# Hybrid encoder trunk, layer 0: where modulation steps and the key's products stand, and how many units of w_out stay plain

## The chip, the cores and the metric

The kernel runs on one core of a Trainium2 chip. The metric is the device time of one execution in microseconds (us). Below, TensorE is the matmul engine (PE, with PEld for its weight loads), VectorE is DVE, ScalarE is ACT, GpSimd is POOL, and SP issues the DMAs. SBUF is the memory on the chip in which all operands lie, PSUM the one that matmuls write.

## The reference

Two layers work on 256 positions of 2048 features. Each layer has this form:

```
mod = silu(c) @ w_mod[l] + b_mod[l]          # six rows of 2048: shift, scale, gate, twice
h = layer_norm(x) * (1 + scale_m) + shift_m
proj = h @ w_in[l]                           # 4288 columns, parts of four mixers
y = concat(y_a, y_b, y_c, y_d)               # gMLP, latent attention, short conv, long conv
x = layer_norm(ALPHA * x + (1 + gate_m) * (y @ w_out[l])) * g + b
h = layer_norm(x) * (1 + scale_f) + shift_f
x = layer_norm(ALPHA * x + (1 + gate_f) * conv_ffn(h)) * g + b
```

In the attention mixer (y_b), a part of `proj` is a latent for the queries, one for keys and values, and 64 columns for the key's rotary part. The latents are normalised and multiplied by a gain; the key part is turned by cosines and sines: `k_rope = k_r * cos + rotated(k_r) * sin`.

## The kernel before

All matrices are float32. A **plain** (in the code: exact) product multiplies float32 operands as they are; its weights are loaded straight into tiles `wexact` of 512 KB. A **split** product cuts each operand into a high half (a cast to float32r by ScalarE, `whi`, line 390) and a low half (what is left, by VectorE, `wlo`, line 391) and makes three products of them (hi by hi, hi by lo, lo by hi). Its weights first land in a tile `wraw` of 1 MB. The tiles `wexact` of most groups live in the same eight buffers as `whi` and `wlo` (four each, line 93). The tiles `wraw`, the weights of the modulation (`wmod`), the rows of gains and biases (`gb`) and the gMLP's parameters share four buffers of 1 MB (`rawp`, line 92).

In **layer 0** the projection is plain. Its last two groups are B (latents, lines 488 to 519) and C (short conv, lines 412 to 461), each of eight units of two k-tiles; C may load two units ahead. The out stage (`out_proj`, line 607) then multiplies the concatenated mixers by w_out in three column chunks: 1024 columns in eight units of two k-tiles (chunk 0), then 512 and 512 columns in four units of four k-tiles each (chunks 1024 and 1536, by their first column). In layer 0 the chunks 1024 and 1536 are plain, and of chunk 0 the first `PLAIN_UNITS` units (line 736). In the last chunk all products of the first 128 positions come ahead of those of the other 128, so that the first tile's norm (line 665) runs beside the second tile's products. That norm needs two rows `gb`, loaded with the last unit's weights (`gains`, line 643), and sums of one of them, made by ScalarE.

**The modulation** is made by VectorE, beside everything else. Each step loads 1 MB of w_mod and takes one instruction over 128x2048 (line 194 for shifts and scales, line 205 for gates). The steps stand in one stream (`mods`, line 305) in a fixed order. A pace sets how many come at a time: each unit adds the rate of its phase (`RATES`, line 35) to a credit, and takes as many steps as the credit has whole parts (`pump`, line 314). The steps of layer 0's feed-forward shift and scale are the last that the out stage's end needs.

**The order.** SP issues all DMAs in one order; an engine runs its instructions in one order; both orders are fixed when the program is built, by a scheduler that takes the instructions in the order of the code as far as their inputs and buffers are ready in its own estimate of the time. `add_manual_dep` adds a fixed order between two instructions. In `run` (line 547) a unit's load is issued before the products of the unit before it, then come the products, the pump and some background pieces (`bg`). The end of group B (`mix_b`, line 1009) squares and copies the latents, and takes `MODS_AHEAD` steps at once (line 1025). The attention (`attend`, line 1062) begins one unit later: it turns the latents on TensorE (`ps_q`, `ps_kv`), makes the key's two products with cosines and sines on VectorE (`kc`, lines 1085 and 1086) and the scaled latents (`kvr`, line 1090). The first of the two kc, and both kvr, are ordered behind the last of the `MODS_AHEAD` steps (`behind`, line 1066). TensorE then adds the key's two products (`ps_kr`) and makes the queries (`ps_qn`). Two PSUM buffers are shared by all these small products (`msp`, line 99), so ps_qn takes over the buffer that the two kvr have read. Beside this the long convolution of mixer D runs: ScalarE scales (line 876), VectorE adds (`convD`, line 879).

Of the kernel before, what the change touches and what calls it, by code (L numbers as in the profile page):

```python
# [9 lines left out]
AF = mybir.ActivationFunctionType  # L10
ALU = mybir.AluOpType
# [4 lines left out]
S = 256  # L16
# [9 lines left out]
C_UV, C_Q, C_SB, C_SC, C_AG = 0, 1024, 1728, 2240, 3264  # L26
# [6 lines left out]


RATES = [
    dict(B=1.3, attend=1.3, C=1.9, out=1.0, out_next=1.55, out_last=0.0, up=0.7, down=0.7, down_next=0.7, down_last=0.0),
    dict(D=1.0, U=0.0, V=0.0, B=0.0, C=0.0, E=0.9, attend=0.0, out=0.6, out_next=0.6, out_last=0.0, up=0.3, down=0.7, down_next=0.7, down_last=0.0),
]

STEPS = [  # L40
    dict(B=1, C=6, out=2, up=2),
    dict(U=7, B=4, C=4, E=8, out=0, up=2),
]

PLAIN_UNITS = 2

MODS_AHEAD = 3

BATCHES = ((0, 4), (4, 4), (8, 4), (12, 4))

# [36 lines left out]
def encoder_kernel(ctx: ExitStack, tc: tile.TileContext, A: dict, consts: bass.AP, out: bass.AP):  # L87
    nc = tc.nc
    pe, act, dve, pool = nc.tensor, nc.scalar, nc.vector, nc.gpsimd
# [41 lines left out]
    sinT = cst[:, 768:1024]  # L131
# [50 lines left out]


    MOD = {}
    last_step = [None]
    data_dep = mybir.DependencyInfo(mybir.DependencyClass.Sync, mybir.DependencyReason.DATA)
    order_dep = mybir.DependencyInfo(mybir.DependencyClass.NoSync, mybir.DependencyReason.DATA)

# [11 lines left out]
    def mod_step(acc, w, kt, first):  # L200
        col = cact[:, kt : kt + 1]
        if first:
            i = dve.tensor_scalar(out=acc, in0=w, scalar1=col, scalar2=None, op0=ALU.mult)
        else:
            i = dve.scalar_tensor_tensor(out=acc, in0=w, scalar=col, in1=acc, op0=ALU.mult, op1=ALU.add)  # L205
        held(i, "mod")
        last_step[0] = i.ins.name

    def gate_rows(l, m, acc):

# [115 lines left out]


    pending = []
    postponed = []
    background = []  # L330

# [189 lines left out]
    hN, first = [], []  # L521
# [22 lines left out]
        for u in range(KT // 4):  # L544
            pump()

    def run(g, ahead=0):
        units, load, products, end, bg = g
        loaded = []

        def get(u):
            while len(loaded) < min(u + 1 + (ahead if u > 0 else 0), units):
                loaded.append(load(len(loaded)))
            return loaded[u]

# [51 lines left out]
    def out_proj(l, stage, w, src, order, gate_of, name, post_g, post_b, before, then, plain=(), bg=0):  # L607
# [112 lines left out]
        for c0, width in CHUNKS:  # L720
            last = c0 + width == D
            nk = 2048 // width
            units = nkt // nk
# [8 lines left out]
            def load_unit(u, c0, width, nk, units, last):  # L732
                kt = order[nk * u]
                assert order[nk * u : nk * u + nk] == list(range(kt, kt + nk))
                spare = nk if last and units - 4 <= u < units - 2 else 0
                exact = c0 in plain or (bool(plain) and u < PLAIN_UNITS)
                parts = weights(w, kt, nk, c0, width, exact, spare)
                s4 = src(kt // 4)
                if exact:
                    return parts, [(s4[:, kt % 4 + k, :], None) for k in range(nk)]  # L740
# [55 lines left out]
    def mixers(l, w_in, Y, hF=None, first_mod=None, quarter=None):  # L796
# [265 lines left out]
        def attend(WQ, WKV, lat, q01, rr):  # L1062
# [20 lines left out]
            by = turn(ps, S, [lat[t][:, 256:320] for t in range(2)])  # L1083
            kc = tmp_tile("kc")
            behind(dve.tensor_tensor(out=kc[0:64, 0:S], in0=by[0:64, :], in1=cosT[0:64, :], op=ALU.mult))
            dve.tensor_tensor(out=kc[0:64, S : 2 * S], in0=by[0:64, :], in1=sinT[0:64, :], op=ALU.mult)
            ps = ms_tile("ps_kv")
            for j in range(2):
                by = turn(ps, j * S, [lat[t][:, j * P : (j + 1) * P] for t in range(2)])
                behind(dve.tensor_scalar(out=kvr[:, j, :], in0=by, scalar1=KVG(j), scalar2=None, op0=ALU.mult))  # L1090

            rope = slot("rope").rearrange("p (j s) -> p j s", j=4)
            ps = ms_tile("ps_kr")
# [211 lines left out]
    def by_blocks(l, w_in, hF, first_mod, quarter, mix_d, mix_u, gelu_v, mix_v, mix_b, mix_c, mix_e):  # L1305
# [94 lines left out]
            mix_c(cps, tps)  # L1400
            mix_e(sumE, None)

        run(group(w_in, C_SC, 1024, f"C{l}", mix_ce, hF=hf, bg=STEPS[l]["C"]), 2)


    def ffn_up(l, G):
# [280 lines left out]
```

## Time and profile before

| | |
|---|---|
| three runs | 2218.09, 2219.70, 2219.76 us; median 2219.7 |
| the profiled execution | 2218.06 us, its span 2216.3 us |
| mean granted clock of TensorE | 0.998 |
| busy: TensorE, VectorE, ScalarE | 2192.1, 1716.9, 1092.7 us |
| moved by the DMA engines | 603.96 MB, mean 273 GB/s |

The span is the time from the first to the last instruction that the profiler saw. A row of a timeline gives the start, the duration of the group, engine, line, operation, output and inputs with their shapes, and how often (x); in brackets stand the idle time of the engine before it and what ended it. A row of stretches gives, for a window of time, its length and the busy time of PE, PEld, DVE, ACT and POOL, each with a count of instructions, then the granted clock, the share of the DMA engines and their GB/s. A row of DMA landings gives the count, the KB of each and the us from issue to landing.

### The profile page before, as it was taken

What the parts mean: (1) busy time and instruction counts of PE and PEld (TensorE: products, weight loads), DVE (VectorE), ACT (ScalarE), POOL (GpSimd) and SP (SyncE); (2) the same over time, 40 slices, a digit from 0 to 9 for tenths busy, and PEclk for the clock granted to TensorE, in tenths of its full rate; (3) what the DMA queues carried; (4) which work ended last, traced back from release to release, by engine and by line L of the source; (5) the groups of instructions that cost most, each with busy time, mean ns of one, the idle gap of its engine ahead of it and who ended that gap; (6) DMA issues with size and microseconds to landing.
All of it is one profiled execution on the core that took longest, in us unless ns stands there. A gap on an engine that the chain in (4) does not pass through costs nothing. (4 is left out here: it accounts for less than half of the span.)

```text
span 2216.3 us, 28397 instructions
## 1 busy us (share of the span) xinstructions
PE 2192.1 (99%) x10880; PEld 1801.1 (81%) x10880; DVE 1716.9 (77%) x2209; ACT 1092.7 (49%) x1677; POOL 21.9 (1%) x38
## 2 busy tenths in 40 slices
PE   9999999999999999999999999999999999999997
PEld 6776875588888888888867988868888888888886
DVE  5658996799888888989968988877766656565776
ACT  3132740655555545545665555465455545454453
POOL 0000000000000000000000000000000000000000
PEclk9999999999999999999999999999999999999999
DMA  9999889588888888888758547856755555555553
GB/s 393 417 374 390 338 330 391 224 331 316 327 315 322 325 328 316 319 329 323 282 208 297 186 156 263 320 197 247 265 210 188 182 198 190 190 190 190 192 192 148
DMA packets 94034, 603.96 MB, mean 273 GB/s; under 512 B 10565, under 2 KB 10693, under 8 KB 29125
## 3 DMA queue, kind: packets, MB, share of 16 engines
q1 hardware_dynamic: 93898, 602.15, 74.0%
q8 instruction: 85, 1.39, 0.2%
q14 instruction: 51, 0.42, 0.1%
HBM read 600.01 MB, written 2.10 MB: 272 GB/s over the span
## 5 line engine op out<-in xcount | busy, mean ns | idle before, releaser
L390 ACT CAST whi<-wraw 128x1024 fp32r<-128x1024 f32 (+1 forms) x608 | 634.5, 1047 | 677.0 <-PE g_c L115 207.8
L391 DVE TENSOR_TENSOR wlo<-wraw,whi 128x1024 fp32r<-128x1024 f32 (+1 forms) x608 | 729.7, 1212 | 285.6 <-ACT whi L390 279.7
L115 PE MATMUL v_c<-hT,whi 128*128 128x512 f32 x1408 | 489.6, 391 | 0.0
L115 PE MATMUL g_c<-hT,whi 128*128 128x512 f32 x1280 | 444.7, 391 | 0.0
L115 PE MATMUL v_c<-hT,wlo 128*128 128x256 f32 x1408 | 394.4, 280 | 0.0
L115 PE MATMUL d<-whi,a 128*128 128x512 f32 x1344 | 386.2, 389 | 0.0
L115 PE MATMUL g_c<-hT,wlo 128*128 128x256 f32 x1280 | 358.4, 280 | 0.0
L194 DVE SCALAR_TENSOR_TENSOR wmod<-wmod,crep 128x2048 f32<-128x2048 f32 x128 | 292.1, 2285 | 45.2 <-DMA wmod<-in_w_mod_dram 44.5
L115 PEld LDWEIGHTS v_c<-hT,whi 128*128 128x128 f32 x1408 | 263.3, 187 | 57.6
L115 PEld LDWEIGHTS d<-whi,a 128*128 128x128 f32 x1344 | 252.2, 188 | 52.2
L115 PEld LDWEIGHTS g_c<-hT,whi 128*128 128x128 f32 x1280 | 239.4, 187 | 52.5
L115 PEld LDWEIGHTS v_c<-hT,wlo 128*128 128x128 f32 x1408 | 266.1, 189 | 0.2
L115 PEld LDWEIGHTS g_c<-hT,wlo 128*128 128x128 f32 x1280 | 241.9, 189 | 0.1
L115 PE MATMUL d<-wlo,a 128*128 128x512 f32 x672 | 232.9, 389 | 0.0
L205 DVE SCALAR_TENSOR_TENSOR macc<-wmod,cact,macc 128x2048 f32<-128x2048 f32 x60 | 140.7, 2346 | 16.1 <-DMA wmod<-in_w_mod_dram 15.7
L115 PEld LDWEIGHTS d<-wlo,a 128*128 128x128 f32 x672 | 126.1, 188 | 26.3
L115 PE MATMUL o<-whi,a 128*128 128x512 f32 x320 | 90.5, 390 | 0.0
L410 DVE TENSOR_TENSOR a<-g,a 128x512 fp32r<-128x512 f32 x132 | 88.6, 682 | 0.0
L534 PE MATMUL first<-wexact,hN 128*128 128x512 f32 x192 | 85.3, 595 | 1.3 <-ACT hN L118 1.0
L409 ACT CAST a<-g 128x512 fp32r<-128x512 f32 x132 | 81.1, 615 | 7.4 <-PE d L115 4.8
L1448 DVE SCALAR_TENSOR_TENSOR u<-g,par,u 128x254 f32<-128x254 f32 (+1 forms) x176 | 74.2, 476 | 0.4 <-ACT u L118 0.2
L115 PEld LDWEIGHTS o<-whi,a 128*128 128x128 f32 x320 | 59.9, 188 | 12.8 <-ACT whi L390 0.4
(321 smaller groups left out, 2379.9 us busy)
## 6 DMA issues: line engine op xcount, KB each, us to landing
wmod<-in_w_mod_dram SPq DMA_DIRECT2D x192, 1024.0 KB, 6.9
wraw<-in_ffn_w_up_dram SPq DMA_DIRECT2D x168, 1024.0 KB, 5.0
wraw<-in_ffn_w_down_dram SPq DMA_DIRECT2D x88, 1024.0 KB, 5.0
wexact<-in_w_in_dram SPq DMA_DIRECT2D x64, 512.0 KB, 9.9
wraw<-in_w_in_dram SPq DMA_DIRECT2D x24, 1024.0 KB, 5.2
wraw<-in_w_out_dram SPq DMA_DIRECT2D x22, 1024.0 KB, 6.3
wexact<-in_w_out_dram SPq DMA_DIRECT2D x20, 512.0 KB, 12.3
wexact<-in_ffn_w_up_dram SPq DMA_DIRECT2D x16, 512.0 KB, 6.5
```

Of the source, the lines that this page charges most:

```text
L115: pe.matmul(o, lhsT, rhs, start=start, stop=stop, skip_group_check=True)
L194: i = dve.scalar_tensor_tensor(out=raw, in0=raw, scalar=1.0, in1=crep, op0=ALU.mult, op1=ALU.mult, accum_out=col)
L205: i = dve.scalar_tensor_tensor(out=acc, in0=w, scalar=col, in1=acc, op0=ALU.mult, op1=ALU.add)
L390: held(act.copy(hi[:, :m], r), "cast")
L391: i = dve.tensor_tensor(out=lo[:, :m], in0=r, in1=hi[:, :m].bitcast(F32), op=ALU.subtract)
L409: act.copy(hi, src)
L410: dve.tensor_tensor(out=lo, in0=src, in1=hi.bitcast(F32), op=ALU.subtract)
L534: i = pe.matmul(ps, hN[kt // 4][:, kt % 4, t * P : (t + 1) * P], parts[kt], start=kt == 0, stop=kt == KT - 1, skip_group_check=True,)
L1448: dve.scalar_tensor_tensor(out=u[:, sh:], in0=x[:, : S - sh], scalar=col(k, j), in1=u[:, sh:], op0=ALU.mult, op1=ALU.add)
```

## The change

1. `RATES` of layer 0: `out` from 1.0 to 0.75, `out_last` from 0.0 to 0.5. Chunk 0 takes six steps instead of eight, chunk 1024 takes seven as before, and the last chunk two instead of none.
2. `PLAIN_UNITS` from 2 to 1: the second unit of chunk 0 is split instead of plain.
3. `MODS_AHEAD` from 3 to 2. The third step is taken in `attend` after the key's second product, and is ordered behind it. The two kvr of layer 0 are made by ScalarE instead of VectorE, with no order behind the steps.
4. The loads of the one plain unit of w_out are issued with C's last unit, one unit earlier than before, and kept in `ready_out` until the out stage takes them.

```diff
-    dict(B=1.3, attend=1.3, C=1.9, out=1.0, out_next=1.55, out_last=0.0, up=0.7, down=0.7, down_next=0.7, down_last=0.0),
+    dict(B=1.3, attend=1.3, C=1.9, out=0.75, out_next=1.55, out_last=0.5, up=0.7, down=0.7, down_next=0.7, down_last=0.0),
...
-PLAIN_UNITS = 2
+PLAIN_UNITS = 1
-MODS_AHEAD = 3
+MODS_AHEAD = 2
...
-        last_step[0] = i.ins.name
+        last_step[0], last_made[0] = i.ins.name, i
...
-    def run(g, ahead=0):
+    def run(g, ahead=0, next_loads=()):
...
                 loaded.append(load(len(loaded)))
+            if u - units + len(next_loads) >= 0:
+                next_loads[u - units]()
             return loaded[u]
...
-                parts = weights(w, kt, nk, c0, width, exact, spare)
+                parts = ready_out.pop(0) if ready_out else weights(w, kt, nk, c0, width, exact, spare)
...
-            dve.tensor_tensor(out=kc[0:64, S : 2 * S], in0=by[0:64, :], in1=sinT[0:64, :], op=ALU.mult)
+            i = dve.tensor_tensor(out=kc[0:64, S : 2 * S], in0=by[0:64, :], in1=sinT[0:64, :], op=ALU.mult)
+            if hF is not None:
+                next(mods, None)
+                tc.add_manual_dep(last_made[0].ins, i.ins.name, order_dep, reason="the key's products come first")
...
-                behind(dve.tensor_scalar(out=kvr[:, j, :], in0=by, scalar1=KVG(j), scalar2=None, op0=ALU.mult))
+                if hF is not None:
+                    act.activation(out=kvr[:, j, :], in_=by, func=AF.Copy, scale=KVG(j))
+                else:
+                    dve.tensor_scalar(out=kvr[:, j, :], in0=by, scalar1=KVG(j), scalar2=None, op0=ALU.mult)
...
-        run(group(w_in, C_SC, 1024, f"C{l}", mix_ce, hF=hf, bg=STEPS[l]["C"]), 2)
+        w_out = (A["w_out"], l)
+        out_first = [lambda u=u: ready_out.append(weights(w_out, 2 * u, 2, 0, 1024, True)) for u in range(PLAIN_UNITS)]
+        run(group(w_in, C_SC, 1024, f"C{l}", mix_ce, hF=hf, bg=STEPS[l]["C"]), 2, out_first)
```

More of the change, by code (lines that the diff above doesn't have):

```diff
@@ L184, in encoder_kernel @@
     MOD = {}
-    last_step = [None]
+    last_step, last_made = [None], [None]
     data_dep = mybir.DependencyInfo(mybir.DependencyClass.Sync, mybir.DependencyReason.DATA)
@@ L328, in encoder_kernel @@
     pending = []
+    ready_out = []
     postponed = []
```

## The prediction

> **What bounds the kernel now.** I read the page first, then TensorE's timeline through layer 0, its stretches table (the busy time of each engine and the granted clock), then the timelines of VectorE, ScalarE and the DMA queue at the places found.
>
> ```profile
> span 2216.3 us, 28397 instructions
> PE 2192.1 (99%) x10880; PEld 1801.1 (81%) x10880; DVE 1716.9 (77%) x2209; ACT 1092.7 (49%) x1677; POOL 21.9 (1%) x38
> ```
>
> TensorE is busy for all but 24 us, so time can only come from its few holes, from a low clock, or from fewer matmul microseconds. The profiled execution took 2218.06 us, 1.8 beyond its span; the three runs gave 2218.09, 2219.70 and 2219.76. All sums below start at 2218.06, 1.6 below the median. The change lies in one stretch, the end of layer 0's projection and its out stage:
>
> ```profile
> 202.76 7.07 PE L115 MATMUL C_c<-hF,wexact 128*128 128x256 f32 x32
> 209.66 0.49 PE L1073 MATMUL ps_q<-cst,lat 128*128 128x128 f32 x3
> 210.50 0.77 PE L1073 MATMUL ps_q<-cst,lat 128*128 128x128 f32 x4 [0.35 <-ACT qg L1079]
> 211.50 0.44 PE L1073 MATMUL ps_kv<-cst,lat 128*128 128x128 f32 x2 [0.23 <-ACT qg L1079]
> 213.35 0.67 PE L115 MATMUL ps_kr<-kc,cst 64*128 64x256 f32 x2 [1.41 <-DVE kc L1086]
> 213.95 0.44 PE L1073 MATMUL ps_kv<-cst,lat 128*128 128x128 f32 x2
> 214.32 0.70 PE L115 MATMUL ps_kr<-kc,cst 64*128 64x256 f32 x2
> 216.31 6.93 PE L115 MATMUL ps_qn<-qg,wq 128*128 128x256 f32 x24 [1.29 <-DVE kvr L1090]
> 223.07 1.46 PE L115 MATMUL ps_qr<-qg,wq 128*128 128x256 f32 x6
> ```
>
> and in the stretches table, where the third figure from the end is the granted clock:
>
> ```profile
> 212.50:216.00 3.50, 1.66 (x6) 0.79 (x6) 3.50 (x6) 0.91 (x3) 0.00 (x0) 0.99 0.99 399
> 216.00:219.40 3.40, 3.10 (x7) 2.53 (x8) 3.40 (x3) 2.67 (x7) 0.00 (x0) 0.51 1.03 406
> ```
>
> Two holes of 1.41 and 1.29 us, both ended by VectorE, leave TensorE busy for 1.66 us of 3.5, and the next 3.4 us run at half clock. Price of that: the 24 ps_qn matmuls take 223.07 - 216.31 = 6.76 us, while 32 of the same width in the first row take 209.66 - 202.76 = 6.90, or 0.216 each, so 5.17 for 24. The low clock costs 1.6 us.
>
> What VectorE was doing:
>
> ```profile
> 205.23 7.32 DVE L205 SCALAR_TENSOR_TENSOR macc<-wmod,cact,macc 128x2048 f32<-128x2048 f32 x3 [8.20 <-DMA wmod<-in_w_mod_dram]
> 212.46 0.41 DVE L1085 TENSOR_TENSOR kc<-ps_q,cst 64x256 f32<-64x256 f32 x1
> 212.80 0.41 DVE L1086 TENSOR_TENSOR kc<-ps_q,cst 64x256 f32<-64x256 f32 x1
> 213.13 0.47 DVE L1090 TENSOR_SCALAR kvr<-ps_kv,par 128x256 f32<-128x256 f32 x1
> 213.52 2.33 DVE L205 SCALAR_TENSOR_TENSOR macc<-wmod,cact,macc 128x2048 f32<-128x2048 f32 x1
> 215.78 0.47 DVE L1090 TENSOR_SCALAR kvr<-ps_kv,par 128x256 f32<-128x256 f32 x1
> 221.70 1.19 DVE L879 TENSOR_TENSOR convD<-convD,scaled 128x988 f32<-128x988 f32 x1 [2.09 <-ACT scaled L876]
> ```
>
> and ScalarE beside it:
>
> ```profile
> 210.98 0.47 ACT L1079 ACTIVATE qg<-ps_q,par 128x256 f32<-128x256 f32 x1 [0.17 <-PE ps_q L1073]
> 215.05 0.36 ACT L1098 COPY rope<-ps_kr 64x256 f32<-64x256 f32 x1 [3.60 <-PE ps_kr L115]
> ```
>
> **Key products.** Three modulation steps stand ahead of kc, a fourth between the two kvr. With two ahead, VectorE is free at 205.23 + 2/3 x 7.32 = 210.1; kc's input is complete at 210.50 + 0.77 = 211.3. The two products take 213.13 - 212.46 = 0.7, so they end at 212.0 and ps_kr starts at 212.1 instead of 213.35. The kvr go to ScalarE, which idles 3.60 us there and does the same shape in 0.47 (the qg row). The second ps_kv then ends 1.25 earlier, at 213.1, its kvr at 213.7, and ps_qn starts near 213.8: **2.5 us** earlier. TensorE would be busy nearly 3 of the 3.5 us to 216.0, so I also count the low clock as gone: **1.6 us**.
>
> The Trainium skill (TensorE: Matmul & The Clock Gate, section "Why this matters for your kernels") asks for no idle gaps over about 3 us. The rows disagree: no gap passes 1.41 us here, and still a half-busy 3.5 us was enough. By the page the clock would not have fallen at all and nothing would come back from it.
>
> The moved step's weights are now issued behind the six C loads, and so land later. The added order makes this step wait for the second product; behind it on VectorE stand convolution taps and further steps, and the taps' reader on TensorE is the mean at the end of C. The step lies beside the taps, where VectorE idles 2.09. Without that cover it costs VectorE up to its 2.33.
>
> **One plain unit.** TensorE's timeline in chunk 1024 and where it meets unit 2's low half, and one piece of the chain that ended last (fp32r products of the same width, undisturbed):
>
> ```profile
> 313.03 0.73 PE L115 MATMUL o<-wlo,a 128*128 128x512 f32 x2
> ...
> 346.44 7.03 PE L115 MATMUL o<-wexact,ya 128*128 128x512 f32 x16
> ...
> 360.17 7.03 PE L115 MATMUL o<-wexact,yc 128*128 128x512 f32 x16
> ```
>
> ```profile
> 1965.47 239.41 PE d L115 x1056
> ```
>
> VectorE: its busy time from 288 (third busy figure of the row), two of its low halves with the step ahead of the first, and the group of activation splits (mean 682 ns):
>
> ```profile
> 288.00:341.20 53.20, 53.05 (x214) 38.49 (x213) 51.25 (x67) 22.94 (x32) 0.70 (x1) 1.00 0.88 337
> ```
>
> ```profile
> 309.55 2.28 DVE L194 SCALAR_TENSOR_TENSOR wmod<-wmod,crep 128x2048 f32<-128x2048 f32 x1
> ...
> 311.76 2.35 DVE L391 TENSOR_TENSOR wlo<-wraw,whi 128x1024 fp32r<-128x1024 f32 x2
> ...
> 338.84 2.35 DVE L391 TENSOR_TENSOR wlo<-wraw,whi 128x1024 fp32r<-128x1024 f32 x2
> ```
>
> ```profile
> L410 DVE TENSOR_TENSOR a<-g,a 128x512 fp32r<-128x512 f32 x132 | 88.6, 682 | 0.0
> ```
>
> Two plain units take 360.17 - 346.44 us, one 6.87. A split unit is 24 matmuls at 239.41 / 1056 = 0.227, 5.44 us. TensorE saves **1.4 us**. On TensorE alone the change is worth 2.5 + 1.6 + 1.4 = 5.5, to 2212.5.
>
> But this stretch isn't TensorE's alone: VectorE is busy for 51.25 of the 53.20 us from 288.0 (288.00 row). Units of chunk 0 are counted from 0. Unit 2's low half runs at 311.76 to 314.1, and TensorE's first matmul on it starts at 313.03; the last unit's is made at 338.84 to 341.2, while chunk 0 ends at 346.44, one split unit after 341.0. VectorE sets the pace. The new split unit adds 2.35 (two low halves) + 0.68 (one pair of activations) = 3.0 to it ahead of unit 2. What is taken off: two kvr (0.94), the idle 2.09 at 221.70 if ScalarE's earlier start fills it, while the wait for kc from 210.1 to 211.3 adds 1.2. The two modulation steps (2.3 each) don't come off there: working the credit through with rate 0.75 from the 0.80 left at the end of C, the units with no step are the fourth and the eighth. So the low half of unit 2 comes 3.0 - 0.9 - 2.1 + 1.2 = 1.2 **later**, and TensorE takes it up at about 314.2. From there TensorE has 22 x 0.227 + 5 x 5.44 = 32.2 us to do, and took 346.44 - 313.03 = 33.4 before; the step left out at the fourth unit pays for VectorE's lag, so I take 32.2 plus a few tenths for the small matmuls between: chunk 0 ends near 346.7, no earlier than now. The 5.5 us are given back while TensorE waits for VectorE. Bounds of this term: nothing lost (5.5 gained), and 33.4 again (1.2 lost).
>
> **First unit of w_out earlier.** The DMA queue's row and TensorE's:
>
> ```profile
> 289.02 0.86 SPq L374 DMA_DIRECT2D wexact<-in_w_out_dram  x2
> ...
> 296.79 13.47 PE L115 MATMUL o<-wexact,ya 128*128 128x512 f32 x31
> ```
>
> It was issued 7.8 us ahead of its use, behind five modulation loads; it goes ahead of two of them, whose loads then come one unit's transfer (1 MB) later on the same queue; their steps are among those VectorE is behind with anyway, so I price that at nothing, with the 2.5 us of a 1 MB load (worked out below) as the upper bound. TensorE does not wait for it now (this row has no idle time), so this is worth nothing by itself; it keeps a TensorE that is up to 4 us early from waiting there.
>
> **Two steps in the last chunk.** Rows of the DMA queue and its landings, the stretches table (last three figures: clock, DMA share, GB/s) and three engines:
>
> ```profile
> 373.15 0.33 SPq L647 DMA_DIRECT2D gb<-in_post_mix_b_dram  x1
> ```
>
> ```profile
> gb<-in_post_mix_b_dram SPq DMA_DIRECT2D x1, 1024.0 KB, 13.5
> ```
>
> ```profile
> 374.00:387.90 13.90, 13.90 (x34) 6.17 (x33) 5.03 (x9) 1.20 (x4) 0.00 (x0) 1.00 1.02 413
> ```
>
> ```profile
> 386.70 0.63 ACT L655 ACTIVATE junk<-gb 128x512 f32<-128x512 f32 x1 [46.97 <-DMA gb<-in_post_mix_b_dram]
> ...
> 387.90 0.69 DVE L637 TENSOR_TENSOR yg<-o,gate 128x512 f32<-128x512 f32 x1 [8.87 <-PE o L115]
> ...
> 398.82 1.52 ACT L118 ACTIVATE xn<-x,rs_o0r 128x512 f32<-128x512 f32 x2 [1.15 <-DVE rs_o0r L715]
> ...
> 401.37 1.04 PE L590 MATMUL ps_xT<-cst,xn 128*128 128x128 f32 x8
> ```
>
> VectorE has 8.87 idle us before 387.90, room for two steps. Their 1 MB loads do not: the DMA engines are full (413 GB/s), so each adds 1.05 MB / 413 = 2.5 us to what follows. The credit puts one after the second unit, ahead of the bias row gb, and one after the fourth, behind gb. The bias row then lands at 373.15 + 13.5 + 2.5 = 389.2, and ScalarE's sums of it, for which VectorE's norm waits, come 2.5 late. The first xn is ready at 398.82 + 0.76 = 399.6, and TensorE wants it at 401.37: 1.8 us of slack. Cost **0.7**, with bounds 0 and, if the second step runs inside the norm, 0.7 + 2.3 = 3.0.
>
> **Sum.** 2218.06, chunk 0 0.3 later (346.7 for 346.44), less 0.7 for small VectorE waits it may recover after 224 (an estimate; bounds as above), plus 0.4 for the norm as the middle of 0 and 0.7: **2218.0**, 0.08% below the median. A measurement of this kernel can hardly tell 0.2% (4.4 us) from no change.
>
> **Rivals.**
> *All of TensorE's gain survives.* VectorE's order is set at build time; if it puts unit 2's low half ahead of one modulation step, the low half comes 1.2 - 2.3 = 1.1 earlier instead, and if two steps slip, 3.4 earlier, which covers most of the 5.5. Time 2212.5 to 2215. For it: modulation steps have no reader before the last chunk's norm. Against: unit 2's low half (311.76) stands right behind such a step (309.55), whose load was issued before unit 2's. Chance 0.26.
> *The key products do not move.* Two further steps, issued by the pace and tied to nothing, come before kc in the program; if one runs at 210.1, kc stays at 212.5, and only kvr's wait goes. The loss in chunk 0 is then the same or less: about 2218 to 2220. Against it: the fourth step did run behind kc. Chance 0.12.
> *The last step stands ahead of the norm.* It lands behind gb, at 389.2 + 2.5 = 391.7. If VectorE has it before yg (387.90), yg waits for it to end at 394.0, 6.1 late; less the slack of 1.8, TensorE idles 4.3 us at 401.37, the half-busy stretch brings 3.4 us of half clock (1.7): 2218.06 + 6.0 = 2224.1, 2225 with the 1.2 of chunk 0. It decides when the load lands after about 385.5 and the order has it first; landing by then it is free. Chance 0.12.
>
> **Numbers.** Forecast 0.50, together with the second rival 0.62 within 0.2%; faster 0.26; slower 0.12. The range 2212.5 to 2222.5 takes in the gain of 5.5 and the norm's 3.0 with 1.2 of chunk 0, and leaves out about 2 in 10, mostly above.
>
> **What would show it.** Key step right: ps_kr near 212, ps_qn near 214, no half clock after it. Pace right: VectorE without idle from 288 to 341, TensorE waiting for wlo in the second and third units, and plain chunk 1024 still starting near 346. Last chunk: gb landing near 389, and a short wait before ps_xT near 401. A chunk 1024 that starts at 341 to 343 would make the forecast wrong on the fast side; a modulation step directly ahead of yg, on the slow side.

## The result, and the profile after

| | before | after |
|---|---|---|
| median, five runs each | 2219.58 us (2218.09 to 2219.76) | 2227.83 us (2227.28 to 2228.08) |
| ratio, 95% interval | | 1.0036 (1.0025 to 1.0047): slower by about a third of a percent |
| profiled execution, span | 2218.06, 2216.3 us | 2227.28, 2225.5 us |

The forecast was 2218.0 with a range up to 2222.5; the time lies 5 us above the range. The profiled executions differ by 9.2 us. TensorE's timeline of the changed kernel, at the places that answer to the rows of before (316.31, 296.79, 313.03, 346.44, 401.37):

```profile
214.29 5.45 PE L115 MATMUL ps_qn<-qg,wq 128*128 128x256 f32 x24
...
292.21 1.89 PE L115 MATMUL ps_mean<-convD,ones 128*128 128x256 f32 x8
293.94 7.03 PE L115 MATMUL o<-wexact,ya 128*128 128x512 f32 x16
305.63 3.57 PE L115 MATMUL ps_var<-ones,sqD 128*128 128x1 f32 x16 [4.66 <-ACT sqD L916]
311.13 1.22 PE L115 MATMUL ps_rD<-dgD,ones 128*128 128x256 f32 x2 [1.93 <-DVE dgD L935]
311.79 2.27 PE L115 MATMUL o<-whi,a 128*128 128x512 f32 x4
314.07 0.80 PE L115 MATMUL o<-wlo,a 128*128 128x512 f32 x2
...
319.72 0.62 PE L115 MATMUL o<-wlo,a 128*128 128x512 f32 x2
...
351.67 7.03 PE L115 MATMUL o<-wexact,ya 128*128 128x512 f32 x16
...
408.88 1.63 PE L593 MATMUL ps_xT<-cst,xn 128*128 128x128 f32 x8 [2.11 <-ACT xn L118]
...
426.38 1.04 PE L593 MATMUL ps_xT<-cst,xn 128*128 128x128 f32 x8
```

and three rows of before that were not shown: the small products of mixer D's norm (`norm_d`: variance, then its inverse root spread over the partitions) in chunk 0, and the third ps_xT.

```profile
310.52 1.84 PE L115 MATMUL ps_var<-ones,sqD 128*128 128x1 f32 x16
319.06 0.59 PE L115 MATMUL ps_rD<-dgD,ones 128*128 128x256 f32 x2
417.23 1.04 PE L590 MATMUL ps_xT<-cst,xn 128*128 128x128 f32 x8
```

Read the differences from top to bottom: w_out's unit 0 starts 2.85 us sooner (293.94 for 296.79), chunk 1024 5.23 later (351.67 for 346.44), the third ps_xT (TensorE's turning of the normalised rows xn) 9.15 later. So **the key's part gains 2.85, chunk 0 loses 8.1, the end of the last chunk 3.9**; nothing else in the span matters. In chunk 0 TensorE ends its one plain unit at 301.0, and the next products in its order, ps_var, start at 305.63: they wait for the squares `sqD`, which ScalarE makes from rows that VectorE has centred. In before, ps_var stood behind two plain units, and ps_rD among unit 3's products, and neither waited. The row at 319.72 is TensorE's first product with unit 2's low half (at 313.03 in before).

VectorE of the changed kernel in the same stretch; rd, dgD and the rows of convD behind ps_rD are that norm:

```profile
291.80 1.37 DVE L1240 TENSOR_TENSOR chC<-C_c,sc 128x512 f32<-128x512 f32 x2
...
299.65 2.29 DVE L194 SCALAR_TENSOR_TENSOR wmod<-wmod,crep 128x2048 f32<-128x2048 f32 x1
...
302.28 2.29 DVE L194 SCALAR_TENSOR_TENSOR wmod<-wmod,crep 128x2048 f32<-128x2048 f32 x1
...
304.49 1.08 DVE L910 SCALAR_TENSOR_TENSOR convD<-ps_mean,convD 128x256 f32<-128x256 f32 x3
305.49 2.28 DVE L194 SCALAR_TENSOR_TENSOR wmod<-wmod,crep 128x2048 f32<-128x2048 f32 x1
...
309.24 0.16 DVE L929 TENSOR_SCALAR rd<-ps_var 128x2 f32<-128x2 f32 x1 [1.46 <-PE ps_var L115]
...
310.59 0.48 DVE L935 TENSOR_SCALAR dgD<-cst,rd 128x128 f32<-128x128 f32 x2 [0.59 <-POOL rd L145]
...
312.46 0.42 DVE L946 TENSOR_TENSOR convD<-convD,ps_rD 128x256 f32<-128x256 f32 x1 [0.79 <-PE ps_rD L115]
312.80 2.35 DVE L392 TENSOR_TENSOR wlo<-wraw,whi 128x1024 fp32r<-128x1024 f32 x2
...
318.27 2.35 DVE L392 TENSOR_TENSOR wlo<-wraw,whi 128x1024 fp32r<-128x1024 f32 x2
```

The centred rows (L910), whose squares TensorE wants at 301.0, are four: the first stands between the two steps of 299.65 and 302.28, the other three behind both. They are done at 305.5, sooner than in before (308.4); but there TensorE came to ps_var only at 310.52. Then the norm's three round trips over TensorE and GpSimd stand ahead of the low halves: VectorE is idle for 1.46 + 0.59 + 0.79 = 2.84. The first split unit's low half is made at 312.80, where before made unit 2's (311.76); unit 2's comes at 318.27. In before, rd stood behind unit 2's low half:

```profile
316.24 0.15 DVE L926 TENSOR_SCALAR rd<-ps_var 128x2 f32<-128x2 f32 x1
```

The stretches table of the changed kernel (the third figure from the end is the granted clock; before had 1.00 in the last two windows, 0.91 in the first):

```profile
205.00:225.00 20.00, 18.00 (x84) 14.37 (x83) 16.53 (x14) 13.48 (x34) 0.40 (x2) 1.00 1.01 415
300.00:320.00 20.00, 13.40 (x51) 10.39 (x50) 17.16 (x26) 9.63 (x14) 1.01 (x1) 0.74 0.65 221
395.00:420.00 25.00, 22.84 (x62) 10.78 (x61) 19.27 (x48) 14.03 (x33) 2.54 (x3) 0.93 0.64 241
```

At 0.74, about half of the 20 us ran at half clock. Chunk 0's loss is then 4.66 + 1.93 of waits, less the 1.4 of the split unit, and the other 2.9 of 8.1 are put down to the half clock as a remainder (ps_var, for one, took 3.57 us for 1.84).

### The profile page after: what moved, and what is told of

The parts are those of the page before. It is cut to its first block, busy times and chain, and to the rows that moved or that the text cites. A ratio compares the mean times of both kernels' runs of the same rounds, so it can differ in the third digit from the quotient of the medians.

```text
span 2225.5 us, 28415 instructions
## 1 busy us (share of the span) xinstructions
PE 2194.1 (99%) x10888; PEld 1804.6 (81%) x10888; DVE 1719.0 (77%) x2210; ACT 1096.6 (49%) x1682; POOL 20.3 (1%) x38
## 5 line engine op out<-in xcount | busy, mean ns | idle before, releaser
L194 DVE SCALAR_TENSOR_TENSOR wmod<-wmod,crep 128x2048 f32<-128x2048 f32 x128 | 292.2, 2286 | 45.9 <-DMA wmod<-in_w_mod_dram 44.9
L115 PE MATMUL o<-whi,a 128*128 128x512 f32 x336 | 95.6, 393 | 0.0
```

Source lines behind the costliest of these rows:

```text
L115: pe.matmul(o, lhsT, rhs, start=start, stop=stop, skip_group_check=True)
L194: i = dve.scalar_tensor_tensor(out=raw, in0=raw, scalar=1.0, in1=crep, op0=ALU.mult, op1=ALU.mult, accum_out=col)
```

## The experiments

Each group of up to four shared a chip with runs of the kernel before; a ratio is to those, with its 95% interval, five rounds. Times of different groups are best compared by their ratios. The diffs show only the changed parts of lines, and `...` stands for what is left out. "Old rates" are 1.0 and 0.0 for `out` and `out_last`. The theories' letters stand for: **T** unit 1, split, stands behind the norm's small products; **P** VectorE's throughput sets chunk 0, as predicted; **L** the last chunk's two steps; **E** the early loads change the order; **K** the key's part does; **K2** the early loads make the raw weights of the split units land late; **G** the half clock; **F** the first low half sets the end; **V** VectorE's queue, with its idle time, does; **I** the order of the two tiles.

### Parts undone, and one plain unit alone

The changed kernel with two plain units:

```diff
-PLAIN_UNITS = 1
+PLAIN_UNITS = 2
```

> The changed kernel with two plain units again, all else as changed. Theory T (order): the new split unit stands on TensorE behind the small matmuls of mixer D's norm, which wait for ScalarE; 8.1 us are lost there. Without that unit the loss goes, the last step inside the first tile's norm stays (3.9): 2218.1 - 2.9 (key products, seen at unit 0) + 3.9 = 2219, at most 2 more if the first split unit (now unit 2) waits too. Theory P (pace, as in the prediction): VectorE has 3.0 us less before unit 2, chunk 0 ends 3 us earlier than in the changed kernel: 2225. Theory L (the last chunk's loads cost it): 2226 to 2228, hardly changed.

Measured 2231.59, 1.0051 (1.0038 to 1.0063): no better than the changed kernel.

The changed kernel with the old rates:

```diff
-out=0.75, out_next=1.55, out_last=0.5
+out=1.0, out_next=1.55, out_last=0.0
```

> The changed kernel with the rates of before (eight steps in chunk 0, none in the last chunk), one plain unit. T: chunk 0 loses its 8.1 us again, the norm of the first tile loses nothing: 2227.8 - 3.9 = 2224. P: the two steps return to VectorE at the fourth and eighth unit, chunk 0 ends 2 to 4 us later than in the changed kernel: 2226 to 2228. L: 2219 or less.

Measured 2225.72, 1.0026 (1.0016 to 1.0037). ps_var still waits 4.67 for sqD; the first ps_xT waits no more, and from chunk 1024 (353.11) to the third ps_xT (423.90) it is 70.79 us, as in before (346.44 to 417.23), where the changed kernel took 74.71.

Both edits together, which leaves the key's part and the early loads (of two units):

> The changed kernel with two plain units and the rates of before: the key products and the early load of w_out alone. T: the 2.9 us that unit 0 gained stay if the order of the norm's small matmuls does no harm: 2215.2; if they wait ahead of unit 2, 1 to 2 us less of gain. P: VectorE sets the pace in chunk 0, its lead there is about 2: 2216 to 2218.

Measured 2226.70, 1.0035 (1.0021 to 1.0048). TensorE and ScalarE:

```profile
307.81 1.84 PE L115 MATMUL ps_var<-ones,sqD 128*128 128x1 f32 x16
311.27 1.22 PE L115 MATMUL ps_rD<-dgD,ones 128*128 128x256 f32 x2 [1.61 <-DVE dgD L935]
318.59 1.22 PE L115 MATMUL o<-whi,a 128*128 128x512 f32 x2 [6.09 <-ACT whi L391]
```

```profile
313.80 1.58 ACT L948 ACTIVATE yd<-convD,par 128x256 f32<-128x256 f32 x3 [9.26 <-DVE convD L946]
...
317.51 1.98 ACT L391 CAST whi<-wraw 128x1024 fp32r<-128x1024 f32 x2
```

The kernel before with `PLAIN_UNITS = 1` alone:

> The kernel before with one plain unit and nothing else. Its order on TensorE puts the first four products of unit 1 ahead of the norm's small matmuls and the rest behind them. T: TensorE waits there for ScalarE's squares, as in the changed kernel but with no key gain: chunk 0 ends 4 to 8 us later, 2222 to 2226. P: 3.0 us more on VectorE, 1.4 less on TensorE: 2219 to 2221.

Measured 2228.92, 1.0038 (1.0025 to 1.005).

```profile
309.08 2.07 PE L115 MATMUL o<-whi,a 128*128 128x512 f32 x4 [5.60 <-ACT whi L390]
```

This one constant costs as much as the whole change. TensorE ends unit 0 at 303.5 and waits 5.60 for unit 1's whi, whose cast stands on ScalarE behind the first of the squares. Chunk 0 takes 59.3 us (296.45 to 355.75) where before took 49.65; the key's part, the early loads and the new rates are all absent from this kernel.

T falls as the whole cause: with two plain units the changed kernel has no split unit 1 behind the norm, and loses no less. In its place the first split unit's cast stands in ScalarE's queue behind yd, the norm's end, which waits for VectorE. But one plain unit alone costs as much. The parts don't add up: one plain unit alone, and the early loads of two units, each leave TensorE 4 to 8 us without work between 300 and 319.

### Key part against early loads

Key part alone, with two plain units and the old rates:

```diff
-        run(group(w_in, C_SC, 1024, f"C{l}", mix_ce, hF=hf, bg=STEPS[l]["C"]), 2, out_first)
+        run(group(w_in, C_SC, 1024, f"C{l}", mix_ce, hF=hf, bg=STEPS[l]["C"]), 2)
```

> The changed kernel with only its key part: the key's products moved, ScalarE scaling kvr, one step made after the key's products; two plain units, the old rates, and w_out's first loads issued where they were. The first theory (all loss in chunk 0 came with the one plain unit) has fallen: the key part with the early loads and two plain units took 2226.7. Theory E (early loads): with w_out's first loads issued ahead, the planner writes the norm's ps_var and ps_rD ahead of the first split unit on TensorE, and that unit's casts behind the norm's yd on ScalarE; without them the order of chunk 0 is that of before. So chunk 0 keeps its length, the key part's 2.8 us stay: 2216.0 to 2217.5, no half clock at 214 and none in chunk 0, and no wait over 2 us between the units. Theory K (the key part alone upsets chunk 0): 2224 to 2228, with the 6 us wait for whi. Theory P of the prediction (VectorE sets chunk 0's end): 2218 to 2220, the 2.8 us wait for wlo.

Measured 2219.10, 1.0002 (0.9993 to 1.0011).

```profile
215.35 7.96 PE L115 MATMUL ps_qn<-qg,wq 128*128 128x256 f32 x24
...
298.27 14.00 PE L115 MATMUL o<-wexact,ya 128*128 128x512 f32 x32 [1.78 <-DMA wexact<-in_w_out_dram]
312.11 1.84 PE L115 MATMUL ps_var<-ones,sqD 128*128 128x1 f32 x16
314.79 0.73 PE L115 MATMUL o<-wlo,a 128*128 128x512 f32 x2 [0.27 <-DVE wlo L392]
```

The early loads of both plain units, with the old rates and with kc and kvr as in before. `MODS_AHEAD` stays 2 and the step that `attend` takes is left out, so this kernel has made one step less than before from there on:

```diff
-            if hF is not None:
-                next(mods, None)
-                tc.add_manual_dep(last_made[0].ins, i.ins.name, order_dep, ...)
...
-                if hF is not None:
-                    act.activation(out=kvr[:, j, :], in_=by, func=AF.Copy, scale=KVG(j))
-                else:
-                    dve.tensor_scalar(out=kvr[:, j, :], ...)
+                behind(dve.tensor_scalar(out=kvr[:, j, :], ...))
```

> The changed kernel with only its early loads: w_out's first two plain units issued during the last units of C, nothing moved at the keys (one step's write and the two steps ahead as the changed kernel has them), two plain units, the old rates. Theory E: ps_var and ps_rD stand ahead of the first split unit and TensorE waits 6 us or more for the round trip and the casts, with 10 to 14 us of half clock behind it: 2226 to 2231. Theory K: the early loads cost nothing by themselves: 2218.5 to 2220.5, with chunk 0 as before.

Measured 2229.30, 1.0049 (1.0036 to 1.0061).

```profile
310.32 1.84 PE L115 MATMUL ps_var<-ones,sqD 128*128 128x1 f32 x16
316.30 1.22 PE L115 MATMUL ps_rD<-dgD,ones 128*128 128x256 f32 x2 [4.14 <-DVE dgD L935]
...
319.24 0.84 PE L115 MATMUL o<-wlo,a 128*128 128x512 f32 x2
...
411.62 2.91 PE L535 MATMUL first<-wexact,hN 128*128 128x512 f32 x3 [3.22 <-ACT hN L118]
```

Not all of this is the early loads: chunk 1024 starts 6.0 later than in before (352.43), and another 4.8 are lost behind it (75.59 us to the third ps_xT for 70.79), where the step that is still owed runs at 408.51 and holds up hN, the input of the feed-forward. The clean comparison is the kernel with the key's part and the early loads (1.0035) against the key's part alone (1.0002), which differ in the early loads only; chunk 1024 starts at 354.50 and 348.20.

So E: with the early loads of two units the scheduler writes ps_rD ahead of the first split unit (319.06, in unit 3, before). The key's part alone leaves the order and chunk 0's pace (33.41 us from 314.79 to chunk 1024 at 348.20; before 346.44 - 313.03 = 33.41), and its time is that of before: in P's range, and E's 2216 to 2217.5 was too low. P's mechanism is not seen here, though: it asks for a wait of 2.8 for wlo, and there is one of 0.27. In this execution the gain went ahead of chunk 0. The key's stretch ran at a granted clock of 0.83 (205 to 225; the 24 ps_qn took 7.96 us), so ps_mean came only 0.45 sooner than in before (294.61 for 295.06), and unit 0 then waited 1.78 for its weights, which were not loaded early.

### Order and clock in the changed kernel

ps_var behind unit 1's last product:

```diff
+                        if hF is not None and t == 0 and j == 0:
+                            tc.add_manual_dep(i.ins, unit_end[("out", l, 2, 1)], order_dep, ...)
```

> The changed kernel with one order added: the first ps_var product stands behind the last product of unit 1. Nothing else. Theory E in the form 'place on TensorE': unit 1's products no longer wait behind the norm's two round trips (4.7 us for sqD, 1.9 us for dgD); but its own casts come at 306 to 308 and its wlo behind a step, so TensorE still waits about 5 us for them: 2222 to 2225, and ps_rD waits for nothing. If the cause is the place alone: 2219 to 2221 (the 6.6 us gone, the norm's 2.3 us stay). If neither the place nor the round trips matter (VectorE's pace): 2227 to 2228, as the changed kernel.

Measured 2229.19, 1.0047 (1.0034 to 1.0059): none of the three. The wait moves to unit 1's casts (6.26 for whi, then 1.73 for wlo), which stand behind the squares on ScalarE.

22 added products behind unit 0's last one:

```diff
+                for _ in range(22 if hF is not None else 0):
+                    i = mm(ps[:, 128:256], ident, ident, True, True)
+                    tc.add_manual_dep(i.ins, unit_end[("out", l, 2, 0)], order_dep, ...)
```

> The changed kernel with 22 products of 128 x 128 added into columns of ps_var's tile that nothing reads, placed behind unit 0's last product, where TensorE waits 4.7 us for sqD: added work, nothing left out. They fill that wait. Theory G (part of the loss is the half clock of 10.2 us that follows it): no half clock in chunk 0, the norm's products, ps_rD and unit 1's first products run at full speed: 3 to 4 us faster than the changed kernel, 2224 to 2225. If the clock is of no account because the waits set the pace: 2227 to 2228. If the added products run over the wait's end: up to 2229.

Measured 2227.68, 1.0043 (1.003 to 1.0057), as the changed kernel. Half clock came all the same, later: 0.83 in 300 to 320. Inconclusive on what the clock is worth.

### Whose queue sets the end of chunk 0

The rates alone on the kernel before:

> The kernel before with the changed kernel's three rates alone (0.75 and 0.5 in place of 1.0 and 0.0), so the two steps run in the last chunk. Chunk 0 keeps its order and its end near 346. Theory L (a step stands inside the last tiles' finish on VectorE, as at 397.05 of the changed kernel, and holds the norm back by 2.3 us; TensorE then waits 2.1 us for xn and runs 3.4 us at half clock): 2222 to 2224.5. Theory P of the prediction (only the bias row's late landing, 0.7): 2219 to 2221.

Measured 2221.84, 1.0011 (1.0002 to 1.002). Chunk 1024 starts at 346.05, hardly earlier for the two steps less, and the last chunk loses what it loses in the changed kernel (74.70 us from there to the third ps_xT, 70.79 in before):

```profile
403.26 1.82 PE L590 MATMUL ps_xT<-cst,xn 128*128 128x128 f32 x8 [2.12 <-ACT xn L118]
```

Key part, early loads, two plain units, old rates, and ps_var two slots later and behind unit 2's products:

```diff
-                steps = none * 15 + steps[:3] + none + steps[3:4] + none + steps[4:]
+                steps = none * 15 + steps[:2] + none * 2 + steps[2:3] + none + steps[3:4] + none + steps[4:]
```

> The kernel of the key part with the early loads, two plain units and the old rates (2226.7), with one order changed: the norm's ps_var stands behind the products of the first split unit (unit 2), and is put into the program two slots later. Theory F: over ten kernels, the plain chunk at 1024 starts 33.2 to 34.7 us after TensorE's first product with a low half, if six split units are left, so chunk 0 ends when VectorE makes the first low half; the early loads cost 6 us because rd, dgD, yd stand ahead of it. With them behind it, VectorE's queue ahead of it holds only its steps and casts: first low half near 312, chunk 1024 at 346 to 347.5: 2217 to 2219.5. Theory K2 (the early loads hold up the raw tiles, so the raw weights land late whatever the order): 2224 to 2227.

Measured 2222.22, 1.0022 (1.0013 to 1.0031), where 1.0035 (1.0021 to 1.0048) was measured without the order: the intervals overlap, and F's range is not reached.

```profile
311.19 1.99 ACT L392 CAST whi<-wraw 128x1024 fp32r<-128x1024 f32 x2 [7.21 <-DMA wraw<-in_w_out_dram]
```

The first split cast now waits for its raw weights, as K2 says (it ran at 309.00 in before), and TensorE waits 3.56 for it. So with two units loaded early the order is not the only cost.

The same with unit 0's load alone early:

```diff
-        out_first = [lambda u=u: ready_out.append(...) for u in range(PLAIN_UNITS)]
+        out_first = [lambda u=u: ready_out.append(...) for u in range(1)]
```

> As the kernel of the key part and the early loads with ps_var behind unit 2's products, but only unit 0's weights are issued early, unit 1's where they were. Theory F: the first low half near 312 again, nothing waits for unit 0's weights (1.8 us without any early load): 2216.5 to 2219. Theory K2: half of the 7 us of loss stays, 2221 to 2223.

Measured 2222.83, 1.0018 (1.0009 to 1.0027). That is in K2's range, but here the first split cast waits only 0.80 for its weights. TensorE waits 3.06 for wlo, which stands behind a step on VectorE, and VectorE then stands 6.17 us at rd, so late is ps_var.

The same, no step with units 0 to 2:

```diff
+                if (stage, l, c0) == ("out", 0, 0):
+                    pace["rate"] = 0.0 if u < 3 else 1.6
```

> As the kernel with unit 0's early load and ps_var behind unit 2's products, and with no modulation step issued in units 0 to 2 of chunk 0, 1.6 for each unit from the fourth on (as many in all). Theory F with VectorE's queue as the cause: two steps of 2.3 us fewer ahead of the first low half, so it comes near 307.5 to 308.5, TensorE has no wait there and chunk 1024 starts at 341.5 to 345, the later end if the steps then hold up the later low halves (6.7 us of VectorE for a unit of 5.4): 2213 to 2217.5. If the first low half doesn't set the end: 2218 to 2220.

Measured 2223.55, 1.0021 (1.0012 to 1.003).

```profile
309.50 0.72 PE L115 MATMUL o<-wlo,a 128*128 128x512 f32 x2 [0.18 <-DVE wlo L393]
...
332.25 1.22 PE L115 MATMUL o<-whi,a 128*128 128x512 f32 x2 [3.31 <-ACT whi L392]
```

F falls: the first low half came 3.5 us before that of the kernel before, and chunk 1024 started at 351.59. The steps that were put off met the norm's rows in units 3 to 5.

### The order of before, set by hand

On top of the key part, unit 0's early load, two plain units and the old rates: ps_var behind unit 1's last product, and on VectorE rd (`i` below) behind unit 2's low half

```diff
+                if hF is not None:
+                    tc.add_manual_dep(i.ins, lo_of[("out", l, 0, 2)], order_dep, ...)
```

> Key part, unit 0's early load, two plain units, old rates, with two orders set: ps_var behind the last plain product, and on VectorE rd behind unit 2's low half, which is the order of the kernel before. Theory F fell: an early first low half (309.5) left chunk 1024 at 351.6. Theory V: chunk 0 ends with VectorE's last low half (4.4 to 8.4 us after its end in all kernels), which is VectorE's work since chC plus the idle time that rd, dgD and the rows behind ps_rD put into its queue (1.5 us before, 4 to 9 us in all slower ones). Here the idle is 1.5 to 2 again and there is one step more than before (2.3): last low half at 338.5 to 341, chunk 1024 at 345.5 to 348, 2217.5 to 2220.5. If the idle is not from that order: 2221 to 2224.

Measured 2220.60, 1.0002 (0.9993 to 1.0011).

```profile
312.78 1.22 PE L115 MATMUL o<-wlo,a 128*128 128x512 f32 x2 [1.85 <-DVE wlo L394]
```

The loss of chunk 0's order is gone, and so is the gain: TensorE comes 2.5 us sooner to unit 0 (294.32), waits 1.85 for VectorE, runs at half clock behind that (0.83 in 300 to 320), and starts chunk 1024 at 347.72.

The same, with the rate 0.75 and two steps in the first two units of the last chunk:

```diff
-out=1.0, out_next=1.55, out_last=0.0
+out=0.75, out_next=1.55, out_last=1.0
...
+                if last and u == 2:
+                    pace["rate"] = 0.0
```

> As the kernel with rd behind unit 2's low half, and the rate 0.75 in chunk 0, whose two steps less are made with the first two units of the last chunk. Theory V: VectorE has two steps of 2.3 us less ahead of its last low half, so TensorE alone sets chunk 0: from unit 0 at 294 to 296, 13.7 + 1.8 + 0.6 + 6 x 5.44 = 48.8, chunk 1024 at 343 to 345; the last chunk as before: 2215 to 2218. If those steps' 1 MB loads hold up the last chunk's weights or the bias row: 2218 to 2221.

Measured 2225.62, 1.0027 (1.0018 to 1.0036): chunk 1024 at 346.25, and a worse last chunk (below).

The changed kernel with rd behind unit 2's low half:

> The changed kernel with one order set on VectorE: rd (and so dgD and the rows behind ps_rD) behind unit 2's low half. ps_var stays ahead of unit 1 on TensorE. Theory V: the 2.9 us that VectorE stood idle for rd, dgD and ps_rD go, unit 1's low half comes near 309 in place of 312.8 and unit 2's 5 us sooner: chunk 1024 at 347 to 349 in place of 351.7, 2223 to 2225.5. If TensorE's own order (ps_var ahead of unit 1, 4.7 us of wait) sets the end: 2226.5 to 2228.

Measured 2227.87, 1.0036 (1.0023 to 1.0049).

```profile
306.00 3.58 PE L115 MATMUL ps_var<-ones,sqD 128*128 128x1 f32 x16 [4.66 <-ACT sqD L919]
309.44 2.05 PE L115 MATMUL o<-whi,a 128*128 128x512 f32 x4
...
351.51 7.03 PE L115 MATMUL o<-wexact,ya 128*128 128x512 f32 x16
```

V alone falls, and the lateness of the low halves is not what sets the end here: VectorE had unit 1's low half at 309.28 and unit 2's at 313.76, 4.5 sooner, and chunk 0 ended where it did. Behind 309.44 TensorE waits only 0.72 us; its seven split units, partly at half clock, set the end. What is left of chunk 0's loss is TensorE's own wait for the squares (4.66) and the clock behind it.

### The last chunk

The changed kernel with both steps early in the chunk:

```diff
-out=0.75, out_next=1.55, out_last=0.5
+out=0.75, out_next=1.55, out_last=1.0
...
+                if last and u == 2:
+                    pace["rate"] = 0.0
```

> The changed kernel with its two last steps made with the first two units of the last column chunk (rate 1.0 there, then 0) instead of the second and the fourth. As many steps, no more work. Theory L (the 2.3 us step at 397.05 stands between the last tiles' finish and their norm): both steps are done before the last yg, the norm comes 2.3 us sooner and the 3.4 us of half clock behind the wait go: 2223 to 2225.5, no wait ahead of ps_xT. If the loss at the last chunk is from the bias row's place behind the steps' loads: 2226 to 2228.

Measured 2230.40, 1.0047 (1.0033 to 1.006): L falls. VectorE's row `yg` of the first tile's last block (its products times the gate), in the changed kernel and here:

```profile
395.72 0.69 DVE L640 TENSOR_TENSOR yg<-o,gate 128x512 f32<-128x512 f32 x1 [9.36 <-PE o L115]
...
397.05 2.29 DVE L194 SCALAR_TENSOR_TENSOR wmod<-wmod,crep 128x2048 f32<-128x2048 f32 x1
```

```profile
400.27 0.69 DVE L640 TENSOR_TENSOR yg<-o,gate 128x512 f32<-128x512 f32 x1 [10.36 <-PE o L115]
```

From chunk 1024's start that is 41.46 us in before (387.90), 44.05 in the changed kernel and 47.48 here (400.27 - 352.79), each time waiting for TensorE. TensorE's rows of the last chunk give its products in this order (tile: products; a plain product is two matmuls in the trace):

```
before                  0: 16   1: 16
changed                 0: 8    1: 3    0: 8    1: 13
steps early             0: 4    1: 4    0: 4    1: 3    0: 8    1: 9
```

A plain product takes 0.86 us (eight in 6.87). Three of tile 1 between those of tile 0 are 2.6, seven are 6.0: the differences above. The changed kernel with tile 1 behind tile 0 again:

```diff
+                        if tail is not None and t == 0:
+                            tail[:] = [m.ins.name]
+                        elif tail:
+                            tc.add_manual_dep(m.ins, tail[0], order_dep, ...)
```

> The changed kernel with one order set in the last column chunk: every product of token tile 1 stands behind the last product of tile 0, as in the kernel before. Nothing else. Moving the two steps within the chunk made it slower (2230.4), so theory L falls in its first form. Theory I (tile order): with steps in the last chunk the planner puts products of tile 1, 0.86 us each, between those of tile 0 (three in the changed kernel, seven with the early steps), so tile 0's finish starts 2.6 or 6.0 us later and its norm ends after TensorE's products. Here the last yg of tile 0 comes 41.5 us after chunk 1024's start instead of 44.05, the norm ends before TensorE does although a step still stands in it, the 2.1 us wait for xn and the half clock behind it go: 2223.5 to 2225. If the step in the norm is what counts: 2226.5 to 2228.

Measured 2226.66, 1.0028 (1.0016 to 1.0039): the wait for xn falls to 0.22, with the step still inside the norm, and the granted clock is 1.00 in 395 to 420.

```profile
355.11 5.31 PE L115 MATMUL o<-wexact,ya 128*128 128x512 f32 x12
...
410.43 1.36 PE L593 MATMUL ps_xT<-cst,xn 128*128 128x128 f32 x8 [0.22 <-ACT xn L118]
```

From chunk 1024 to ps_xT 55.3 us, 54.9 before and 57.2 in the changed kernel: I holds for the wait. To the third ps_xT it is 72.02, so 2.7 of the 3.9 are back, with the step still inside the norm. In time it is not told apart from the changed kernel (1.0036, 1.0025 to 1.0047), and it came out above I's 2223.5 to 2225. The profiled execution, the slowest of the seven at 2229.23, lost 3.4 us more ahead of chunk 1024, where the code is the same (the last section); what the others lost there was not traced.

All of it at once, to get the gain out: the orders of the last two parts, and chunk 0's rate 0 for units 0 and 1, then 1.0.

> All orders set at once: key part, unit 0's early load, two plain units, ps_var behind the last plain product, rd behind unit 2's low half, tile 0's products ahead of tile 1's in the last chunk; no step in units 0 and 1 of chunk 0, one with each of the other six, two with the first two units of the last chunk. Theory V with the waits named: one step less ahead of the first low half (near 309 instead of 311.3), so TensorE waits for nothing in chunk 0 and there is no half clock: chunk 1024 at 343 to 344.5, the last chunk as before: 2214.5 to 2216.5, faster than both. If the last low half still sets the end: chunk 1024 at 346 and 2217 to 2219. If the two steps' loads hold up the last chunk: over 2219.

Measured 2220.64, 1.0003 (0.9994 to 1.0011): no version beats the kernel before. Chunk 0 has no wait over 0.83 us, and chunk 1024 starts at 345.26, 1.2 sooner than before. The last chunk takes it back:

```profile
390.96 0.69 DVE L648 TENSOR_TENSOR yg<-o,gate 128x512 f32<-128x512 f32 x1 [8.41 <-ACT junk L666]
...
403.21 1.36 PE L596 MATMUL ps_xT<-cst,xn 128*128 128x128 f32 x8 [0.99 <-ACT xn L118]
```

```profile
381.35 3.70 PE L115 MATMUL o<-wexact,yc 128*128 128x512 f32 x8 [1.21 <-DMA wexact<-in_w_out_dram]
```

Here yg waits for ScalarE's sums of the bias row, which begin 44.9 us after chunk 1024 (40.3 in before), as the row landed behind the two steps' loads: the cost that the prediction feared (0.7, bounds 0 and 3.0). TensorE also waits 1.21 for the chunk's own weights.

## Why the prediction was wrong

- **What bounds it: right.** The key's two holes and the half clock behind them were real, and the change removed them in the profiled execution. ps_kr did not come to 212.1 but to 213.23, since both ps_kv pairs now stand ahead of it with two waits of 0.56 for ScalarE's kvr. ps_qn came 2.0 sooner (2.5 predicted), at full speed. Unit 0 was 2.85 us sooner, 4.1 predicted. That the half clock went was in part luck: in half of the profiled executions with this stretch it came back (the last section), while the sum counted its 1.6 as sure. No run shows the 0.7 that the sum takes off for VectorE waits behind 224. That the key's gain is given back to VectorE, as forecast, shows in the kernel with the order of before set by hand (1.85 of wait for wlo); in the kernel with the key's part alone, also 1.0002, it had gone ahead of chunk 0.
- **One plain unit: here it failed.** The step was that unit 2's low half comes 1.2 later and TensorE "takes it up at about 314.2". TensorE took it up at 319.72. From there its products took 31.95 us, as the sum's prices have it (20 x 0.227 + 5 x 5.44 = 31.7), so the pace of the split units was right, and the loss lies ahead of unit 2. The sum took the order of both engines from the kernel before and added VectorE's 3.0 us to it. It had no term for when the new split unit 1 could start on TensorE.
- What stood there was the norm of mixer D, which has no line in the diff. Two plain units are 13.7 us that need nothing from VectorE; in before they covered the wait for the squares. With one, TensorE was at ps_var at 301.0, waited 4.66 for the squares and 1.93 for dgD, and lost 2.9 more, put down to half clock. Unit 1 started at 311.79 and chunk 1024 at 351.67, 5.2 later than in before and 4.0 beyond the bound of 1.2. That the one plain unit does this by itself is shown by the kernel before with that constant alone (1.0038).
- VectorE was late as well: unit 2's low half came 6.5 later (318.27 for 311.76), though VectorE ended C 2.86 sooner (291.80; chC was at 294.66). Ahead of it now stood, beside the 3.0 us that were priced, the norm's rd, dgD and rows (2.1 us) with their 2.84 of idle time, and one step more (2.3). That lateness did not set the end: with rd behind unit 2's low half this came at 313.76, and chunk 1024 started at 351.51 all the same.
- **"First unit of w_out earlier":** a price of nothing, at most 2.5, was too low for two units, whose early loads cost 6.3 us at chunk 1024 (354.50 for 348.20): they change the scheduler's order, and the raw weights come later. For one unit, as in the changed kernel, no run shows the price alone. The reason given for the early load held: without it, unit 0 waited 1.78 us for its weights.
- **Two steps in the last chunk: 0.7 predicted, 3.9 measured** with what follows it. The bias row did not land late in the changed kernel (ScalarE's sums began 39.9 us after chunk 1024, 40.3 before). TensorE's own order of tiles moved the norm by 2.6, and the second step ran inside it (2.3, the upper bound's reason). The slower rival had the right place (a step at the last yg, half clock behind it) and came nearest, 2225 at 0.12, but its condition was not what decided.

What stays open: how much of chunk 0's loss is the half clock by itself, since filling the wait only moved it. No run has the changed kernel without its one early load, so its share of the loss is not known. And why the early loads change the scheduler's order was seen in its result, not traced in its estimates.

## What to carry to other kernels

When the order of each engine is fixed at build time from an estimate of the times, a change of loads or pace can, as here, reorder instructions that the diff doesn't name; price an edit by the rebuilt order of each engine around it, not by adding its microseconds to the old one. Before shortening the work of the engine that waits for nothing, look at what cover it gives: here 13.7 us of plain products let VectorE run late. A gain ahead of a stretch that another engine paces can be given back at that engine's first hand-over, as here at the first low half.

## What the runs showed of the hardware

The key's stretch is written alike in the changed kernel and in the fifteen variants that have its key part, and TensorE's waits in it are the same (0.35, 0.23, 0.56 and 0.56 us, to 0.01). Yet it ran at different clocks: the 24 ps_qn took 5.45 us in eight of the sixteen profiled executions, and 6.57 to 8.20 in the other eight. ps_var behind unit 1, with 8.20, had this in 205 to 225 (the changed kernel's row, at 1.00, stands above):

```profile
205.00:225.00 20.00, 18.29 (x70) 14.14 (x70) 13.62 (x9) 11.15 (x27) 0.95 (x3) 0.83 1.02 417
```

A clock of 0.83 over 20 us is 6.8 us at half. At ps_mean this kernel is 2.9 us behind the changed one (295.07 for 292.21), of which 0.6 were there at ps_q (210.83 for 210.22). That is of the size of the key part's whole gain, so one profiled execution could not price it.
